# Sixty-four bytes ahead of the activations: moving the SBUF addresses of a two-block transformer kernel

## The chip, the cores and the metric

The kernel runs on one core of one Trainium2 chip. The metric is the device time of one execution in microseconds (us), as the median of three runs. Differences of well under one per cent matter here, because the runs of the kernel agree within 0.15%.

## The reference: what is computed

Two transformer blocks of two layers each are applied to one sequence of 256 tokens with 1024 channels, in float32:

```
first block, 2 layers:   x = x + rmsnorm(mix1(rmsnorm(x)))    # retention, short conv, 31-tap conv, gated
                         x = x + rmsnorm(ffn1(rmsnorm(x)))    # up 1024 -> 2*2816, conv of 3, silu, down 2816 -> 1024
second block, 2 layers:  x = x + mix2(rms(x))                 # mLSTM, sparse and differential attention, gated
                         x = x + ffn0(rms(x))                 # up 1024 -> 2*2816, silu, down 2816 -> 1024
```

The mixers have a wide input projection, three branches and an output projection. By far the most arithmetic lies in products of weights with activations.

## The kernel before

Activations are kept with channels on the 128 partitions and 256 tokens along the free axis. All weights come as one stream of chunks of 128 x 1024 float32 (`wraw`, line 307, loaded by SyncE's queue, four buffers). TensorE multiplies float32 at a reduced precision in one go (type `float32r`), so each chunk is split into two float32r parts whose sum is exact: ScalarE copies the rounding (`whi`, line 326) and VectorE subtracts it (`wlo`, line 415). Activations are split in the same way into a high and a low part: `yh`/`yl` and `hh`/`hl` for the norms' outputs and branch outputs, `fh`/`fl` inside the feed-forward stages, `ckh`/`ckl` for the key/value rank. Each block of 128 x 128 weights then meets an activation tile in three matmuls, high by high, low by high and high by low, added up in PSUM:

```
todo = [(0, 0), (0, 1), (1, 0)] if len(ws) == 2 else [(0, 0)]
for j, (a, b) in enumerate(todo):
    self.mm(o, ws[a], xs[b], ...)        # mm(out, stationary, moving)
```

In this form (kind "B" of the method `job`) the 128 columns of weights are loaded into the array (LDWEIGHTS) and 256 columns of activations stream past them (MATMUL). The trace calls such a matmul `acc<-hh,whi`: the moving operand stands first, the stationary one second. A few products (kind "A", for the values of the attentions) have the roles changed: 512 columns of weights stream past 128 columns of activations, `acc<-whi,hh`. A few chunks go to TensorE unsplit, as true float32 (`acc<-yw,wraw`), and so do sums over channels (`sp<-sqt,ones`) and the small matmuls of the mixers. Every program matmul in float32 stands in the trace as two.

Tasks of the mixers and norms are interleaved with the products by estimated times of TensorE and VectorE (`side`, `spawn`), and a scheduler sets each engine's order when the program is built.

Memory in SBUF comes from pools that are laid one behind the other, each buffer at the next free byte rounded up to a multiple of 32:

```
self.wpool = ctx.enter_context(tc.tile_pool(name="weights", bufs=1))
self.cpool = ctx.enter_context(tc.tile_pool(name="consts", bufs=1))
self.xpool = ctx.enter_context(tc.tile_pool(name="state", bufs=1))
...
self.x = self.xpool.tile([P, KD, T], F32, name="x")
```

These are lines 352 to 364. In the built program the addresses (bytes in each partition) are as follows; the last column is the start modulo 128:

| pool | buffers | first byte | modulo 128 |
|---|---|---|---|
| weights | `wraw`, `whi`, `wlo`, four each of 4096 bytes | 16,512 | 0, all twelve |
| consts | tables, parameters, `ones` | 65,664 | 0 to 96 |
| state | `x`, `yh`, `yl`, `sqt`, `hh`, `hl`, `mg` | 73,408 | 64, all of them |
| of a feed-forward stage | `fh`, `fl` and temporaries | 131,776 | 64, all of them |
| of a first mixer | `dec` ... `glu`, then `yn`, `c`, ..., then `u`, `gate` | 131,776 | 64, then 32, then 96 |
| of a second mixer | `misc`, then `ckh`, `ckl`, `prob`, ..., then `dq` ... `gate` | 131,776 | 64, then 32, then 0 |

So before the change each activation that streams through TensorE in a large product starts 64 bytes past a multiple of 128 (tiles lie 1024 bytes apart), each weight at a multiple of 128, and `ckh`/`ckl` 32 bytes past one.

Of the kernel before, what the change touches and what calls it, by code (L numbers as in the profile page):

```python
# [11 lines left out]
F32 = mybir.dt.float32  # L12
# [5 lines left out]
P = 128  # L18
# [28 lines left out]
# norms after which the first chunks of weights and what they meet go unsplit  # L47
WHOLE = (1, 2, 3, 4)
# tiles of a product that ends a chain, the last ones apart
COLUMNS = ((0, 2), (2, 2), (4, 2), (6, 1), (7, 1))  # L50
# gates and products of the branches, in their order
# [8 lines left out]
def ffn_up(arr, l):  # L60
    """Gate and value tiles side by side; the first two products take four tiles."""
    t = [[_cols(i * P, P), _cols(FF + i * P, P)] for i in range(KF)]
    return [(arr, (l,), "B", KD, c) for c in [t[0] + t[1], t[2] + t[3]] + t[4:]]


def plan():
    """The weights in the order in which the tensor engine takes them: (array, index, kind,
    k tiles, columns), kind "B" by column tiles of 128 and "A" by rows of 512."""
    jobs = []

    def seg(arr, idx, nk, off, n, step=256):
        for i in range(0, n, step):
            jobs.append((arr, idx, "B", nk, [_cols(off + i + j, P) for j in range(0, step, P)]))

    def last_singly(arr, idx, nk):
        seg(arr, idx, nk, 0, D - 256)
        seg(arr, idx, nk, D - 256, 256, P)

    for l in range(DEPTH):
        seg("w_in", (l,), KD, OFF1["cfb"], 512, 512)  # L80
        seg("w_in", (l,), KD, OFF1["cfa"], 512, 512)
        for s, n in (("q", 256), ("k", 256)):
            seg("w_in", (l,), KD, OFF1[s], n)
        jobs.append(("w_in", (l,), "A", KD, _cols(OFF1["v"], 512)))
        for s, n in (("scc", 512), ("scx", 512), ("scb", 512), ("g", 512)):
            seg("w_in", (l,), KD, OFF1[s], n)
        for what, b in BRANCHES1:
            if what == "g":
                seg("w_in", (l,), KD, OFF1["gate"] + b * D, D)
            else:  # L90
                seg(("w_ret_out", "w_sc_out", "w_cf_out")[b], (l,), 4, 0, D)
        last_singly("w_o", (l,), KD)
        jobs += ffn_up("w_up", l)
        last_singly("w_down", (l,), KF)
    for l in range(DEPTH):
        w = "w_in_2"
        misc = np.full(P, -1)
        misc[:64] = _cols(OFF2["ik"], 64)
        misc[64:72] = _cols(OFF2["mif"], 8)
        misc[72:76] = _cols(OFF2["iw"], 4)  # L100
        jobs.append((w, (l,), "B", KD, [_cols(OFF2[s] + j, P) for s in ("iq", "ckv") for j in (0, P)]))
        seg(w, (l,), KD, OFF2["mqk"], 512, 512)
        jobs.append((w, (l,), "B", KD, [misc]))
        seg(w, (l,), KD, OFF2["mqk"] + 512, 512)
        jobs.append((w, (l,), "A", KD, _cols(OFF2["mv"], 512)))
        seg(w, (l,), KD, OFF2["mo"], 512)
        seg(w, (l,), KD, OFF2["dq"], 512)
        seg(w, (l,), KD, OFF2["dk"], 512)
        jobs.append((w, (l,), "A", KD, _cols(OFF2["dv"], 512)))
        seg("dsa_w_kv_up_2", (l,), 2, 0, 512)  # L110
        jobs.append(("dsa_w_kv_up_2", (l,), "A", 2, _cols(512, 512)))
        seg(w, (l,), KD, OFF2["sq"], 512)
        for what, b in BRANCHES2:
            if what == "g":
                seg(w, (l,), KD, OFF2["gate"] + b * D, D)
            else:
                seg("w_branch_2", (l, b), 4, 0, D)
        seg("w_out_2", (l,), KD, 0, D)
        jobs += ffn_up("w_gate_up_2", l)
        if l + 1 < DEPTH:  # L120
            seg("w_down_2", (l,), KF, 0, D)
        else:
            last_singly("w_down_2", (l,), KF)
    return jobs
# [48 lines left out]
def pack_params(inputs=None):  # L173
    """Per-channel parameters, channels on partitions: (offsets, array)."""
    off, parts = {}, []
# [37 lines left out]
def make_consts():  # L213
    """Tables that depend on shapes alone: (offsets, array [128, n])."""
    off, parts = {}, []
# [55 lines left out]
def whole_chunks():  # L271
    """The chunks that go to the tensor engine as float32, unsplit."""
    out, n, i = set(), 0, 0
    for _, _, kind, nk, cols in plan():
        if kind == "B" and len(cols) == 4:
            if i // 2 in WHOLE:
                out.add(n // CB)
            i += 1
        n += nk * (len(cols) if kind == "B" else 4)
    return out  # L280


class Weights:
    """The stream of weights: loads ahead, then each chunk as the sum of two float32r parts."""
# [13 lines left out]
    def cuts(self, c):  # L298
        """The first chunk comes in halves."""
# [44 lines left out]
class Gen:  # L344
    SLACK = 4000

    def __init__(self, ctx, tc, aps):
# [15 lines left out]
        self.idle = None  # L363
        self.x = self.xpool.tile([P, KD, T], F32, name="x")
# [82 lines left out]
    def split(self, hi, lo, src):  # L447
        """src as the sum of its float32r rounding and of the exact rest."""
# [3 lines left out]
    def behind(self, engine):  # L452
        """What is traced here is issued after the engine's last urgent instruction."""
# [21 lines left out]
    def side(self):  # L475
        """Steps of the tasks beside the products, as far as the vector engine keeps up."""
# [13 lines left out]
    def job(self, evac, mov, needs=(), scale=None, last=False, spare=None):  # L490
        """The next product of the plan. mov(k) gives the two parts of the activations' tile k;
        scale, per token, is for activations that were not normalised yet; spare gives tiles."""
# [3 lines left out]
        if kind == "B":  # L496
            n = len(cols)
            accs = [self.acc() for _ in range(-(-n // 2))]
            if self.idle is not None:
                # only to keep the tensor engine's clock up while it waits  # L500
# [4 lines left out]
            for k in range(nk):  # L505
                xs = mov(k)
                for t in range(n):
# [4 lines left out]
                    # a start clears the marks of its whole bank: the first product of a bank has it  # L512
# [32 lines left out]
    def swap(self, out, src):  # L545
        """src with the halves of each 64 channels exchanged"""
# [3 lines left out]
    def rows(self, r):  # L550
        # r in DRAM, from where a row goes to many partitions
# [4 lines left out]
    def spread(self, out, row):  # L556
        """a row on all the partitions of out"""
        self.nc.sync.dma_start(out, row.to_broadcast(list(out.shape)))

# [31 lines left out]
    def rstd(self, pool, ps, scale, name):  # L591
        """1 / sqrt(scale * ps + eps)"""
# [6 lines left out]
    def sumsq(self, out, last, hold):  # L599
        """Over channels, on every partition: the sum of the squares of the eight tiles, which it  # L600
        takes by pairs, the last two also one by one (send). The first ones are added up before.
        With hold the tensor engine gets them together at the end."""
# [37 lines left out]
    def start_norm(self, g, l, folded=4):  # L640
        """Takes x by pairs of tiles (feed) for a norm whose scale per token comes last."""
# [20 lines left out]
    def end_norm(self, sd=None):  # L662
        """What the first products take, with their scale, and what the others take."""
# [38 lines left out]
    def branches(self, order, bufs, pool, mov, gate_load, needs, ys, done):  # L702
        """The sum over branches of gate * (branch output times its matrix), as two parts. A gate
        sigmoid(z) comes as tanh(z / 2), its double less 1."""
# [31 lines left out]
    def post_norm(self, zg, sums, gpre, l):  # L736
        """x += normalised zg; then the next norm's input. With s the root mean square of z, what
        the norm sees is u = s * x + zg, s times the new x."""
# [23 lines left out]
    def unscale(self, sd):  # L762
        """x out of u"""
# [10 lines left out]
    def out_proj(self, mov, g, l):  # L774
        """Four products whose columns are scaled by g, with the sum of their squares."""
# [11 lines left out]
    def first_mix(self, l, norm):  # L787
        dmov, rs, whole, mov = norm
        nc = self.nc
        with ExitStack() as st:  # L790
# [6 lines left out]
            def new_y(b):  # L797
                """Buffers for a branch's output, once those of the one before last are free."""
# [13 lines left out]
            # conformer convolution  # L812
# [65 lines left out]
            # retention  # L878
# [44 lines left out]
            # short convolution  # L923
# [133 lines left out]
    def residual(self, mov, gpre, l):  # L1057
        """x += four products; then the next norm's input."""
# [17 lines left out]
    def second_mix(self, l, norm):  # L1076
        dmov, rs, whole, mov = norm
        nc = self.nc
        with ExitStack() as st:
# [11 lines left out]
            def new_y(b):  # L1091
                """Buffers for a branch's output, once those of the one before last are free."""
# [14 lines left out]
            def rope(o):  # L1107
                """Rotates two tiles in place."""
# [6 lines left out]
            # indexer  # L1115
# [63 lines left out]
            # key/value rank  # L1179
# [33 lines left out]
            def q_task(sqs, dst, rq):  # L1213
                """rotation of the queries, and their scale per token and head"""
# [39 lines left out]
            # mLSTM queries and keys  # L1254
# [29 lines left out]
            # mLSTM gates  # L1284
# [102 lines left out]
            # attention with a softmax: sets of (queries, keys) of 64 channels  # L1387
            def softmax_group(q, k, rq, t, grp, bias, p, sums):
                """p = exp(scores - max) for the queries of tile t, sums its row sums. A group is
                sets in the same half of the partitions, one a tile."""  # L1390
# [22 lines left out]
            def transposed(p):  # L1413
                """p by keys: for each set its blocks of keys"""
# [18 lines left out]
            def ahead(q, k, rq, t, bias):  # L1433
                """The groups of tile t with their softmax, one group ahead."""
# [49 lines left out]
            def diff(l=l):  # L1484
                init = 0.8 - 0.6 * math.exp(-0.3 * l)
                for t in range(2):
                    yt = tl([P, 512], "yt", tag="yt", bufs=3)
                    for (half, tiles), p, sums in ahead(dq, dk, rq_d, t, None):
# [5 lines left out]
                        # both maps in one, up to the first one's sums  # L1494
# [44 lines left out]
            # differential attention  # L1539
# [22 lines left out]
            # sparse attention: keys and values out of the rank  # L1562
# [72 lines left out]
```

## Time and profile before

| | |
|---|---|
| median of 3 runs (lowest to highest) | 1789.89 us (1788.43 to 1791.16) |
| profiled execution, first to last instruction | 1789.1 us |
| TensorE (PE), matmuls | 1777.4 us busy, 99%, 14462 instructions |
| PE's weight loads (PEld) | 1729.2 us busy, 97% |
| VectorE (DVE) | 1363.0 us, 76% |
| ScalarE (ACT) | 1111.0 us, 62% |
| GpSimd (POOL) | 70.2 us, 4% |
| DMA | 322.52 MB, 180 GB/s in the mean |

The profiled execution's own time is its span; the median of the runs is 0.8 us longer, which covers what lies around the instructions and the scatter of the runs. Matmuls are pipelined, so the duration of one (about 280 ns) says little; what counts is the distance from the start of one to the start of the next. It is read from a long unbroken piece of the chain, as its length divided by its count, or from starts in the timeline.

### The profile page before, as it was taken

The page shows a single profiled execution, that of the slowest core. Times are in us where ns is not written, and L with a number is a line of the kernel's source. Part 1 is how long each engine was busy: PE and PEld are TensorE (multiplying, and loading weights), DVE is VectorE, ACT ScalarE, POOL GpSimd, SP SyncE. Part 2 cuts the span into 40 slices and gives each one's busy share as a digit, 9 for nine tenths or more (in the row PEclk, how much of TensorE's full clock was granted, in tenths as well). Part 3 has the DMA queues.
Part 4 walks back from the last instruction along what each step waited for, and adds up shares of the span by engine and source line. Part 5 has one row for each costly group of instructions (what it writes and reads, how often), then busy time and mean ns, then how long its engine had stood idle before and what let it go on. Part 6 is the DMA issues. An engine that isn't in the chain of part 4 may idle for free.

```text
span 1789.1 us, 35765 instructions
## 1 busy us (share of the span) xinstructions
PE 1777.4 (99%) x14462; PEld 1729.2 (97%) x14462; DVE 1363.0 (76%) x2082; ACT 1111.0 (62%) x1787; POOL 70.2 (4%) x144
## 2 busy tenths in 40 slices
PE   8999999999999999999999999999999999999999
PEld 8999999999999999999998999999999999999999
DVE  8988679865999769884887877865569887677553
ACT  7575468755666567765576666654457666655542
POOL 0000000000000000000022100000000310000000
PEclk9999999999999999999999999999999999999999
DMA  7555546554655546555465644565555664356663
GB/s 265 191 171 179 187 154 200 188 187 164 210 168 188 177 138 204 189 189 188 137 195 177 201 142 139 168 207 194 189 186 180 199 201 139 124 177 200 193 196 132
DMA packets 94648, 322.52 MB, mean 180 GB/s; under 512 B 12257, under 2 KB 16913, under 8 KB 94482
## 3 DMA queue, kind: packets, MB, share of 16 engines
q1 hardware_dynamic: 91010, 314.15, 53.9%
q0 software_dynamic: 3328, 6.09, 1.1%
q8 instruction: 113, 1.85, 0.4%
q14 instruction: 53, 0.43, 0.1%
q10 hardware_dynamic: 144, 0.00, 0.0%
HBM read 312.80 MB, written 1.10 MB: 175 GB/s over the span
## 4 chain that ended last, share of the span: by engine, by line
PE 97%; DVE 1%; DMA 1%; issue 0%; ACT 0%; POOL 0%; SPq 0%; DVEq 0%; ACTq 0%; POOLq 0%
PE acc L403 90%; PE sp L403 6%; PE sp L408 1%; DMA tmp<-dq 0%; DMA Wm<-rows 0%; DMA x<-x 0%; DVE wlo L415 0%; DVE sc L1167 0%; DVE x L415 0%; DVE m L1166 0%; DVE yw L420 0%; ACT sd L445 0%; DVE dq L415 0%; ACT whi L326 0%; POOL tmp L548 0%
## 5 line engine op out<-in xcount | busy, mean ns | idle before, releaser
L326 ACT ACTIVATE whi<-wraw 128x1024 fp32r<-128x1024 f32 (+1 forms) x575 | 606.7, 1057 | 535.9 <-PE acc L403 367.8
L415 DVE TENSOR_TENSOR wlo<-wraw,whi 128x1024 fp32r<-128x1024 f32 (+1 forms) x575 | 699.0, 1220 | 282.9 <-ACT whi L326 281.3
L403 PE MATMUL acc<-hh,whi 128*128 128x256 f32 x2832 | 791.4, 280 | 0.0
L403 PE MATMUL acc<-hl,whi 128*128 128x256 f32 x2832 | 790.8, 280 | 0.0
L403 PE MATMUL acc<-hh,wlo 128*128 128x256 f32 x2832 | 789.9, 280 | 0.0
L403 PEld LDWEIGHTS acc<-hh,whi 128*128 128x128 f32 x2832 | 531.0, 188 | 5.5 <-issue 3.7
L403 PEld LDWEIGHTS acc<-hl,whi 128*128 128x128 f32 x2832 | 531.7, 188 | 1.9 <-issue 1.2
L403 PEld LDWEIGHTS acc<-hh,wlo 128*128 128x128 f32 x2832 | 531.4, 188 | 1.1 <-issue 0.8
L403 PE MATMUL acc<-yh,whi 128*128 128x256 f32 x1280 | 269.7, 284 | 6.2 <-ACT whi L326 6.2
L403 PE MATMUL acc<-yh,wlo 128*128 128x256 f32 x832 | 231.3, 283 | 0.0
L403 PEld LDWEIGHTS acc<-yh,whi 128*128 128x128 f32 x1280 | 210.5, 190 | 7.1 <-ACT whi L326 6.2
L403 PE MATMUL acc<-fh,wlo 128*128 128x256 f32 x704 | 196.0, 278 | 0.0
L403 PE MATMUL acc<-fl,whi 128*128 128x256 f32 x704 | 195.6, 278 | 0.0
L403 PE MATMUL acc<-fh,whi 128*128 128x256 f32 x704 | 195.5, 278 | 0.0
L403 PEld LDWEIGHTS acc<-yh,wlo 128*128 128x128 f32 x832 | 155.8, 189 | 0.4
L403 PEld LDWEIGHTS acc<-fh,wlo 128*128 128x128 f32 x704 | 132.3, 188 | 0.0
L403 PEld LDWEIGHTS acc<-fl,whi 128*128 128x128 f32 x704 | 132.2, 188 | 0.0
L403 PEld LDWEIGHTS acc<-fh,whi 128*128 128x128 f32 x704 | 132.0, 188 | 0.0
L403 PE MATMUL acc<-yl,whi 128*128 128x256 f32 x384 | 108.2, 282 | 0.0
L403 PEld LDWEIGHTS acc<-yl,whi 128*128 128x128 f32 x384 | 72.1, 188 | 0.2
L445 ACT ACT_TABLE_LOAD x50 | 64.2, 1283 | 5.5 <-DVE Wm L426 3.0
L420 DVE SCALAR_TENSOR_TENSOR up<-z,prm,up 128x254 f32<-128x254 f32 (+1 forms) x128 | 55.3, 479 | 0.0
(282 smaller groups left out, 1815.2 us busy)
## 6 DMA issues: line engine op xcount, KB each, us to landing
wraw<-stream SPq DMA_DIRECT2D x581, 512.0 KB, 3.6
kr<-rows SPq DMA_DIRECT2D x32, 64.0 KB, 3.0
dec<-decay SPq DMA_DIRECT2D x2, 768.0 KB, 4.3
x<-x SPq DMA_DIRECT2D x4, 256.0 KB, 6.3
rf<-rows SPq DMA_DIRECT2D x8, 128.0 KB, 3.5
tmp<-dq POOLq DMA_DIRECT2D x16, 64.0 KB, 3.8
Wm<-rows SPq DMA_DIRECT2D x8, 128.0 KB, 3.6
tmp<-dk POOLq DMA_DIRECT2D x16, 64.0 KB, 3.9
```

The source lines that it names most:

```text
L326: nc.scalar.activation(h[:, s], r[:, s], AF.Copy)
L403: return self.nc.tensor.matmul(out, lhsT, rhs, start=start, stop=stop, **kw)
L408: return self.nc.tensor.transpose(out, in_, self.c("ident")[:k, :k])
L415: self.recent = self.nc.vector.tensor_tensor(out=out, in0=a, in1=b, op=op)
L420: return self.nc.vector.scalar_tensor_tensor(out, a, s, b, op0=op0, op1=op1)
L445: return self.nc.scalar.activation(out, in_, f, **kw)
```

## The change

One tile of 16 float32 per partition is put in front of `x`, the first tile of the pool `state`. Nothing reads or writes it. In the built program the address of every buffer of the pool `state` and of all pools behind it is 64 bytes higher: `x` starts at 73,472 instead of 73,408, and the feed-forward and mixer pools at 131,840 instead of 131,776. So `yh`, `yl`, `sqt`, `hh`, `hl`, `mg`, `fh`, `fl` lie at multiples of 128; `ckh` and `ckl` at 96 past one; what stood at 96 now stands at 32, and what stood at 0 in the second mixers (`dq` ... `gate`) at 64. The weights and the constants stay where they are. The instructions of all engines, their order and their waits are the same in both programs, one by one; only addresses differ. The rest of the diff takes out comments and shifts line numbers by two.

```
         self.t_x = [None]
         self.urgent = {}
         self.idle = None
+
+        self.xpool.tile([P, 16], F32, name="pad")
         self.x = self.xpool.tile([P, KD, T], F32, name="x")
```

## Rows read from the trace of the kernel before

**Rows 1.** The page: span, busy time of the engines, the chain by engine.
```profile
span 1789.1 us, 35765 instructions
PE 1777.4 (99%) x14462; PEld 1729.2 (97%) x14462; DVE 1363.0 (76%) x2082; ACT 1111.0 (62%) x1787; POOL 70.2 (4%) x144
...
PE 97%; DVE 1%; DMA 1%; issue 0%; ACT 0%; POOL 0%; SPq 0%; DVEq 0%; ACTq 0%; POOLq 0%
```

**Rows 2.** Groups of matmuls by form: count, busy us, mean ns, idle before.
```profile
L403 PE MATMUL acc<-hh,whi 128*128 128x256 f32 x2832 | 791.4, 280 | 0.0
...
L403 PE MATMUL acc<-yh,whi 128*128 128x256 f32 x1280 | 269.7, 284 | 6.2 <-ACT whi L326 6.2
L403 PE MATMUL acc<-yh,wlo 128*128 128x256 f32 x832 | 231.3, 283 | 0.0
L403 PE MATMUL acc<-fh,wlo 128*128 128x256 f32 x704 | 196.0, 278 | 0.0
...
L403 PE MATMUL acc<-yl,whi 128*128 128x256 f32 x384 | 108.2, 282 | 0.0
...
L403 PE MATMUL acc<-ckh,whi 128*128 128x256 f32 x16 | 4.8, 299 | 0.0
```

**Rows 3.** Chain in order of time, long pieces: start us, us, what.
```profile
169.86 66.31 PE acc L403 x563
...
251.65 177.61 PE acc L403 x1508
...
675.74 177.61 PE acc L403 x1508
...
1150.37 166.84 PE acc L403 x1472
...
1343.51 10.54 PE acc L403 x93
...
1613.05 172.40 PE acc L403 x1521
```

**Rows 4.** Windows: length, busy us (count) of each engine, PE's clock, DMA.
```profile
core 0: us, PE busy (x) PEld busy (x) DVE busy (x) ACT busy (x) POOL busy (x), PEclk, DMA share, GB/s
700.00:800.00 100.00, 100.00 (x852) 100.00 (x851) 88.36 (x152) 78.09 (x144) 0.00 (x0) 1.00 0.59 191
...
1160.00:1260.00 100.00, 100.00 (x885) 100.00 (x884) 62.59 (x84) 51.07 (x78) 0.00 (x0) 1.00 0.63 200
```

**Rows 5.** Timeline of PE across two float32 passes: start us, us, instruction.
```profile
1316.36 0.28 PE L403 MATMUL acc<-fh,wlo 128*128 128x256 f32 x1
...
1316.92 0.28 PE L403 MATMUL acc<-fl,whi 128*128 128x256 f32 x1
1317.04 0.60 PE L403 MATMUL sp<-sqt,ones 128*128 128x256 f32 x2
...
1317.59 0.28 PE L403 MATMUL acc<-fh,whi 128*128 128x256 f32 x1
...
1318.18 0.28 PE L403 MATMUL acc<-fh,wlo 128*128 128x256 f32 x1
```

**Rows 6.** Timeline of PE, moving operand 32 bytes past a multiple of 128.
```profile
967.00 0.28 PE L403 MATMUL acc<-ckh,wlo 128*128 128x256 f32 x1
...
968.78 0.28 PE L403 MATMUL acc<-ckh,wlo 128*128 128x256 f32 x1
```

**Rows 7.** Timeline of PE, weights moving, 512 columns from a multiple of 128.
```profile
45.31 0.40 PE L403 MATMUL acc<-whi,hh 128*128 128x512 f32 x1
...
47.41 0.40 PE L403 MATMUL acc<-whi,hh 128*128 128x512 f32 x1
```

**Rows 8.** Timeline of PE, eleven passes of unsplit float32.
```profile
857.80 2.54 PE L403 MATMUL acc<-yw,wraw 128*128 128x256 f32 x11
```

**Rows 9.** Groups of DVE and ACT by form, 480 to 860 us.
```profile
L415 DVE TENSOR_TENSOR wlo<-wraw,whi 128x1024 fp32r<-128x1024 f32 x123 | 149.9, 1222 | 55.9 <-ACT whi L326 55.6
...
L415 DVE TENSOR_TENSOR c<-c,tap 128x1024 f32<-128x1024 f32 x13 | 15.8, 1218 | 0.0
L445 ACT ACTIVATE z<-acc 128x512 f32<-128x512 f32 x18 | 10.4, 580 | 0.0
L445 ACT ACTIVATE gate<-acc 128x512 f32<-128x512 f32 x12 | 7.0, 579 | 0.0
```

More of the change, by code (lines that the diff above doesn't have):

```diff
@@ L363, in __init__ @@
         self.idle = None
+        self.xpool.tile([P, 16], F32, name="pad")
         self.x = self.xpool.tile([P, KD, T], F32, name="x")
```

## The prediction

> **What bounds the kernel now.** I read the page first. TensorE is busy for 1777.4 of 1789.1 us and the chain that ends last is 97% PE [rows 1]: time can be won or lost only in the distance between one matmul and the next. VectorE is idle for a quarter of the span and ScalarE for more than a third; a change of a per cent in either is absorbed.
>
> The groups by form come next: which matmuls are these? Three products with `hh`/`hl` of 2832 each, `yh,whi` 1280, `yh,wlo` 832, `yl,whi` 384, three with `fh`/`fl` of 704 each and three with `ckh`/`ckl` of 16 each [rows 2]. That is 8496 + 2496 + 2112 + 48 = 13,152 matmuls of 256 columns in float32r. At roughly 117 ns apiece they are about 1,540 us, so a nanosecond more or less in this one distance is 13 us, or 0.7%.
>
> Then I took long pieces of the chain, in which nothing else stands, and divided. Here is what the reader is to see: there are two levels. 177.61 us / 1508 = 117.78 ns, twice over, in both feed-forward stages of the first block, and 66.31 / 563 = 117.78 in its first mixer; but 166.84 / 1472 = 113.34, 172.40 / 1521 = 113.35 and 10.54 / 93 = 113.3 in the second block [rows 3]. It is the same instruction with the same forms. The granted clock is 1.00 (2.4 GHz) in a window of either level, and DMA carries 191 GB/s at the one and 200 GB/s at the other [rows 4], so neither clock nor DMA makes the difference. ScalarE and VectorE are busier where the level is high, 78 and 88 us of 100 against 51 and 63. But the level does not come and go with them within a piece: it steps at a point. In the timeline the five distances from 1316.36 to 1316.92 take 0.56 us, 112 ns each by starts that are rounded to 10 ns; two float32 passes for a sum of squares follow at 1317.04, and from 1317.59 to 1318.18 five distances take 0.59 us, 118 ns each [rows 5]; of each six starts the first and the last are shown. Same tiles `fh` and `fl`, same addresses, same engines beside it. The streams thus have at least two steady rhythms of weight load and matmul, and a break decides into which one they fall.
>
> How far are both from a bound? A float32 pass takes two clocks a column: (2.54 - 0.38) / 10 = 216 ns for 256 columns (0.38 is about the length of the last pass) [rows 8]. Half of it, 108 ns, is what 256 columns need at one clock a column. The split streams lose 5.3 ns at the low level and 9.8 ns at the high one. Something in the reading of operands is not quite free, and it is there that addresses can matter.
>
> **The change, part by part.** No instruction comes, goes or moves, and no wait changes. What changes is one property: moving operands of all 13,104 large products start at 0 modulo 128 instead of 64, with the weights still at 0.
>
> *VectorE and ScalarE.* A subtraction of 128 x 1024 takes 1222 ns with its operands at 0 (`wraw`, `whi`) and 1218 ns at 32 (`c`, `tap`); a copy of 128 x 512 out of PSUM takes 580 ns to `z` at 64 and 579 ns to `gate` at 96 [rows 9]. Within 0.3% the start does not count, and both have idle time to hide that. Cost: nothing. If this cover were gone, 0.3% of 1222 ns on some 570 splits of weights would be 2 us.
>
> *Float32 passes and small matmuls.* `yw` and `sqt` move from 64 to 0. At 216 ns per pass they stand at two clocks a column already [rows 8]. Cost: nothing; no nearer row tells of a loss.
>
> *The streams.* No row shows a stream of 256 columns with both operands at multiples of 128, so this is bounded from both sides. Below: 108 ns, the bound above. With 9,700 matmuls at the high level and 3,270 at the low one that would give 9,700 x 9.78 + 3,270 x 5.34 = 94.9 + 17.5 = 112 us. (The counts: 13,152 less the 1472 + 1521 + 93 in long low pieces is 10,066; I estimate that 370 of these stand beside another kind of work or in short low pieces, nearly half of them in each, so 9,700 high and some 3,270 low.) Above: the only streams with another start, `ckh`/`ckl` at 32, take from 967.00 to 968.78 fifteen distances, 1.78 / 15 = 118.7 ns [rows 6]. This shows that the start is not indifferent: it is above both levels found at 64. All streams at 118.7 would cost 9,700 x 0.92 + 3,270 x 5.36 = 8.9 + 17.5 = 26 us. Between them stands a row of a moving operand at 0, though of another shape and with its stationary operand at 64: nine distances of 512 columns in 2.10 us, 233.3 ns [rows 7], or 116.7 per 256 columns.
>
> Which value? From 32 to 64 the distance goes from 118.7 to 117.8 or 113.3: the rounder start is the faster one, and at 64 the low rhythm already exists and holds for 1521 matmuls without a break. I take it that with both operands at 0 the streams fall into the low rhythm and stay there: 9,700 x (117.78 - 113.34) = 9,700 x 4.44 = 43 us saved. Of the low 3,270 nothing changes.
>
> The Trainium skill speaks against this. Its page "SBUF — State Buffer" (section Specifications (TRN2)) gives 16 bytes as the line of SBUF; by it 32, 64 and 0 would all be as good, since all are multiples of 16, and the sum would be 0. The trace does not quite agree: the fifteen distances at 32 stand above those at 64.
>
> What is late next, once 43 us are gone? ScalarE waits for TensorE and not the other way round in the splits, TensorE's whole wait for `whi` is 6.2 us, at the start [rows 2], and the low level already runs with DMA at 200 GB/s [rows 4]. VectorE's 88.36 us per 852 matmuls would meet a window of 96.5 us: 92% busy, still room. So nothing takes the place.
>
> Sum: 1789.1 - 43 = 1746 us for the span, and with the 0.8 us between span and median 1747 us.
>
> **The rivals.**
>
> *A: nothing happens.* Levels are chosen by the phase in which a stream starts after a break, and one address shows both [rows 5]; 64 bytes may be a whole period of whatever is read. Then every break lands as before, since the instructions are the same: 1790 us. The same time follows if the streams go to the middle value of rows 7, 116.7: 9,700 x 1.1 saved, 3,270 x 3.3 lost, 0 in sum. For it: row by row, what fixes the level is not the start alone. Against it: the streams at 32.
>
> *B: breaks land anew, partly to the good.* If the phases change but both rhythms remain, some of the high pieces become low. Each feed-forward stage of the first block is worth 1508 x 4.44 = 6.7 us, the rest of the high ones 30 us. If the two low stages turn high (2,993 x 4.44 = 13.3 us lost) and all others low, 43 - 13.3 = 30 us are won in sum. So the case spans 1755 to 1785 us, about 1775 if only the two high feed-forward stages turn.
>
> *C: slower, the low rhythm is lost.* The low level stands almost wholly in the two feed-forward stages of the second block, 1472 + 1521 matmuls [rows 3]. If after the shift these start in the high rhythm, as the stages of the first block do, and no other gains, it costs 3,270 x 4.44 = 14.5 us: 1804 us. It decides from the point where more matmuls turn high than low. For it: three quarters of the streams are high now, so the high rhythm is what a break mostly leads to. Against it: for the same reason there is three times more to win than to lose. In the worst of it the streams take the 118.7 of rows 6: 1816 us.
>
> *D: both stalls go* and streams near 108 ns: 1678 us. For it nothing in the rows but that float32 passes reach this rate.
>
> **How the numbers follow.** No change means within 0.2%, 3.6 us, about what can be told apart here. The forecast, nearly all streams low, gets 0.35; B 0.12; D and values between it and the forecast 0.05; A 0.27, its middle value included; C 0.21, of it 0.06 for 118.7 or worse. Faster is 0.35 + 0.12 + 0.05 = 0.52, same 0.27, slower 0.21. The range takes in the forecast with a little below it, B, A and the price of C: 1742 to 1806 us; outside are D (0.05), the worst of C (0.06) and a few per cent for the unknown. Within the forecast's own case it is 1742 to 1754.
>
> **What would show it.** Right: the two long pieces of the first block's feed-forward stages shrink from 177.61 us to 1508 x 113.34 = 170.9 us, those of the second block keep 166.8 and 172.4 us, and the fall in span is 9,700 times the fall per matmul. Wrong: pieces at 117.78 still in the first block (A, B), at 117.78 in the second (C), or a third level; also wrong would be a gain that stands in waits and not in the distance of matmuls, or VectorE and ScalarE groups that change by more than 1%.

## The result

The changed kernel takes 1822.45 us (median of four runs, 1819.98 to 1824.79) against 1790.53 us of the kernel before on the same chip (1788.43 to 1791.22). The ratio is 1.018, 95% interval 1.0168 to 1.0192: it is slower by about 32 us. The forecast of 1747 us had the wrong sign, and the result lies above the range.

### The profile page after: what moved, and what is told of

It is laid out like the page before. It is cut to its first block, busy times and chain, and to the rows that moved or that the text cites. A ratio compares the mean times of both kernels' runs of the same rounds, so it can differ in the third digit from the quotient of the medians.

```text
span 1818.2 us, 35765 instructions
## 1 busy us (share of the span) xinstructions
PE 1807.2 (99%) x14462; PEld 1760.1 (97%) x14462; DVE 1363.9 (75%) x2082; ACT 1110.9 (61%) x1787; POOL 69.3 (4%) x144
## 4 chain that ended last, share of the span: by engine, by line
PE 99%; DVE 0%; ACT 0%; DMA 0%; issue 0%
PE acc L405 92%; PE sp L405 6%; PE sp L410 1%; DMA x<-x 0%; DVE x L417 0%; DVE yw L422 0%; ACT sd L447 0%; ACT yh L447 0%; ACT sqt L447 0%; ACT whi L326 0%
## 5 line engine op out<-in xcount | busy, mean ns | idle before, releaser
L405 PE MATMUL acc<-hl,whi 128*128 128x256 f32 x2832 | 799.5, 283 | 0.0
L405 PE MATMUL acc<-hh,wlo 128*128 128x256 f32 x2832 | 798.9, 283 | 0.0
L405 PE MATMUL acc<-yh,whi 128*128 128x256 f32 x1280 | 273.7, 287 | 6.4 <-ACT whi L326 6.4
```

The lines of the kernel that those rows point to most:

```text
L405: return self.nc.tensor.matmul(out, lhsT, rhs, start=start, stop=stop, **kw)
```

## The profile after

The page first: span, busy time of the engines, and further down the chain by engine (lines of the source are two higher than before).

```profile
span 1818.2 us, 35765 instructions
PE 1807.2 (99%) x14462; PEld 1760.1 (97%) x14462; DVE 1363.9 (75%) x2082; ACT 1110.9 (61%) x1787; POOL 69.3 (4%) x144
...
PE 99%; DVE 0%; ACT 0%; DMA 0%; issue 0%
```

Against [rows 1] the instructions are as many, VectorE and ScalarE are busy as long as before to within 1 us, and TensorE is busy 29.8 us longer in a span that is 29.1 us longer. The time stands in TensorE and nowhere else. The groups of matmuls by form (count, busy us, mean ns, idle before) say that no new wait came, and which forms grew:

```profile
L405 PE MATMUL acc<-hh,whi 128*128 128x256 f32 x2832 | 798.8, 283 | 0.0
L405 PE MATMUL acc<-yh,whi 128*128 128x256 f32 x1280 | 273.7, 287 | 6.4 <-ACT whi L326 6.4
...
L405 PE MATMUL acc<-fh,wlo 128*128 128x256 f32 x704 | 198.8, 283 | 0.0
```

The only idle time before these groups is the 6.4 us at the start, 6.2 before [rows 2]; the mean duration is 3 to 5 ns up. Durations of pipelined matmuls say little, so next comes the chain in order of time (start us, us, what), the same six pieces as in [rows 3]:

```profile
171.64 67.56 PE acc L405 x563
...
254.69 178.95 PE acc L405 x1508
...
682.92 178.95 PE acc L405 x1508
...
1159.45 174.68 PE acc L405 x1472
...
1360.77 11.03 PE acc L405 x93
...
1632.10 182.53 PE acc L405 x1521
```

67.56 / 563 = 120.0 ns, 178.95 / 1508 = 118.67 twice, 174.68 / 1472 = 118.67, 11.03 / 93 = 118.6 and 182.53 / 1521 = 120.0. Before they were 117.78 or 113.34. Both old rhythms are gone, the low one and the high one, and two slower ones stand in their place. Summed over all 12,850 distances from one of these streams to the next, the mean went from 116.63 to 119.08 ns: 2.45 ns x 12,850 = 31.5 us; the rest of the chain is some 2 us shorter, which leaves the 29.1 us.

Clock and DMA are no reason. The windows over the two feed-forward stages (length, busy us and count of PE, PEld, DVE, ACT, POOL, then PE's clock, DMA share, GB/s) show the full clock, 2.4 GHz, as [rows 4] do, and fewer matmuls in 100 us with both engines beside them less busy:

```profile
710.00:810.00 100.00, 100.00 (x845) 100.00 (x844) 87.67 (x152) 76.46 (x139) 0.00 (x0) 1.00 0.56 187
1170.00:1270.00 100.00, 100.00 (x845) 100.00 (x844) 58.92 (x80) 48.95 (x74) 0.00 (x0) 1.00 0.58 190
```

The two float32 passes at which the level had stepped up in [rows 5] stand here at 1333.97 (timeline of PE: start us, us, instruction):

```profile
1333.38 0.28 PE L405 MATMUL acc<-fh,whi 128*128 128x256 f32 x1
...
1333.85 0.28 PE L405 MATMUL acc<-fl,whi 128*128 128x256 f32 x1
1333.97 0.59 PE L405 MATMUL sp<-sqt,ones 128*128 128x256 f32 x2
...
1334.52 0.28 PE L405 MATMUL acc<-fh,whi 128*128 128x256 f32 x1
...
1337.96 0.28 PE L405 MATMUL acc<-fh,wlo 128*128 128x256 f32 x1
```

Four distances of 0.47 us in sum before them are about 118 ns each, and 29 distances of 3.44 us behind them are 118.6: no step here.

What was costed at nothing cost nothing. The 512 columns of moving weights take nine distances from 45.76 to 47.85 us, 232.2 ns each (233.3 in [rows 7]); the unsplit float32 passes (2.97 - 0.38) / 12 = 216 ns, as in [rows 8]:

```profile
45.76 0.39 PE L405 MATMUL acc<-whi,hh 128*128 128x512 f32 x1
...
47.85 0.40 PE L405 MATMUL acc<-whi,hh 128*128 128x512 f32 x1
...
866.11 2.97 PE L405 MATMUL acc<-yw,wraw 128*128 128x256 f32 x13
...
974.57 0.28 PE L405 MATMUL acc<-ckh,wlo 128*128 128x256 f32 x1
...
976.34 0.28 PE L405 MATMUL acc<-ckh,wlo 128*128 128x256 f32 x1
```

The last two rows answer to [rows 6]: fifteen distances in 1.77 us, 118.0 ns, with `ckh` at 96 past a multiple of 128 where 32 past one gave 118.7.

And the groups of VectorE and ScalarE that [rows 9] showed stand within 2 ns of what they were:

```profile
L417 DVE TENSOR_TENSOR wlo<-wraw,whi 128x1024 fp32r<-128x1024 f32 x123 | 149.8, 1220 | 59.0 <-ACT whi L326 58.4
...
L417 DVE TENSOR_TENSOR c<-c,tap 128x1024 f32<-128x1024 f32 x13 | 15.8, 1217 | 0.0
```

```profile
L447 ACT ACTIVATE z<-acc 128x512 f32<-128x512 f32 x18 | 10.4, 579 | 0.0
...
L447 ACT ACTIVATE gate<-acc 128x512 f32<-128x512 f32 x12 | 7.0, 580 | 0.0
```

## The experiments

Theories, as the expectations call them. R: the distance of the moving operand's start from the weights' start decides which rhythms there are. M: the moving operand's own start decides. L: any new layout deals the rhythms anew. Later T and P: what counts is the distance to the weights that are loaded beside the stream, or to the stream's own weights. Ratios are to the kernel before on the same chip, with 95% intervals. "Apart" is the start of the activations less the start of the weights; it is 64 bytes before, modulo 128 and modulo 256 alike, and 128 modulo 256 after.

### Is it the start, or the distance? (e1, e2)

e1 undoes the change and puts the pad ahead of the weights instead, so that activations lie at 0 as after and weights at 64; e2 has both pads, so that nothing is at 0 but the distance is that of after.

```
+        self.wpool.tile([P, 16], F32, name="padw")     # e1 and e2
+        self.xpool.tile([P, 16], F32, name="pad")      # e2 alone
```

> Activations at 0 modulo 128 as in the changed kernel, but the weights moved to 64: the two operands of a matmul lie 64 bytes apart again. Theory R (what counts is the start of the moving operand against that of the weights, modulo 128): the rhythms of the kernel before come back, 113.3 and 117.8 ns, and about 1790 us. Theory M (the moving operand's own start counts, and 0 is bad): 118.7 and 120 ns as after the change, about 1822 us. Theory L (every layout deals the breaks anew, without a law): any time from 1750 to 1825 us, with both of the old rhythms somewhere in it.

> Weights and activations both at 64 modulo 128, so 0 bytes apart. Theory R: 118.7 and 120 ns, about 1822 us. Theory M: as before the change, 113.3 and 117.8 ns, about 1790 us. Theory L: any time from 1750 to 1825 us.

e1: 1790.90 us, ratio 0.9999 (0.9990 to 1.0008). e2: 1826.62 us, ratio 1.0194 (1.0179 to 1.0210). The long pieces of e1's chain:

```profile
251.36 177.61 PE acc L404 x1508
...
675.57 177.61 PE acc L404 x1508
1150.51 166.84 PE acc L404 x1472
```

Their lengths are those of [rows 3] to the last digit, with the activations where after has them. In e2 the same stages take 180.96, 178.95 and 176.64 us (120.0, 118.67 and 120.0 ns). M has fallen: activations at a multiple of 128 are as good as at 64, if the weights stand 64 bytes away. R holds for starts that are moved together by 64, and L has no support, since e1's new addresses dealt every long piece as before. The distance gives the set of rhythms, not each piece's choice among them: e2 has after's distance, and yet two of these three stages are at 120.0 where after had 118.67.

### Other distances (e3, e4, e7)

Pads of 32, 128 and 256 bytes in place of the 64.

```
+        self.xpool.tile([P, n], F32, name="pad")       # e3: n = 8, e4: n = 32, e7: n = 64
```

> Weights at 0, activations at 96 modulo 128 (ahead of them 32 bytes in place of 64). Theory R in its narrow form (only 64 apart is good): 118.7 to 120 ns, 1815 to 1830 us, as the streams with ckh and ckl had at 32. In a wide form (the cost grows with the distance from 64 apart): between, some 1805 us. Theory L: any time from 1750 to 1825 us.

> 128 bytes ahead of the activations in place of 64: they lie at 64 modulo 128 again, but a whole 128 further. Theories R and M with a period of 128 bytes: 113.3 and 117.8 ns and 1790 us, within 0.3%. If the period is 256 bytes or more, the time is another one, as with the 64 bytes some 1822 us. Theory L: any time from 1750 to 1825 us.

> 256 bytes ahead of the activations: 64 modulo 128, and 64 modulo 256 against the weights as before the change (128 bytes had made that 192, and the breaks then led to the low rhythm more often). If the landing of the breaks has a period of 256 bytes: piece by piece the rhythms of before, 1790 us within 0.2%. If it has a longer period: other pieces low, 1770 to 1800 us.

e3 (96 apart): 1832.97 us, ratio 1.0232 (1.0217 to 1.0247); 98% of the streams in long pieces stand at 120.0 ns, one level, the slowest of these runs, and just above the range that narrow R gave. e4 (192 apart): 1783.63 us, ratio 0.9956 (0.9942 to 0.9970), outside the 0.3% that a period of 128 allowed. e7 (320 apart): 1790.29 us, ratio 1.0000 (0.9990 to 1.0009), all pieces as before. So 256 more change nothing, while 128 more keep both rhythms and deal them otherwise. Long pieces of e4's chain:

```profile
667.93 177.61 PE acc L404 x1508
...
1139.91 166.86 PE acc L404 x1472
...
1596.89 179.15 PE acc L404 x1521
```

The last stage went from 113.35 to 179.15 / 1521 = 117.78 ns, and yet more of the shorter pieces are low than before: of some 12,800 matmuls in pieces of twenty or more, about 5,640 are low (3,300 before). This is the prediction's picture of breaks that choose between two rhythms, at a layout where the two exist.

### Which pair of operands? (e6)

e6 moves only the low parts: `wlo` to 64, and `yl`, `hl`, `fl` to 0, by pads between the tiles. Then high by high is 64 apart, and of the other products each is 0 apart (modulo 128; modulo 256 it is 64 or 192, and 0 or 128).

```
+            if not self.parts:
+                self.g.wpool.tile([P, 16], F32, name="padw")   # ahead of the first wlo
 ...                                                            # and pads of 16 around yl, hl, fl
```

> High parts as before the change (weights whi at 0, activations yh, hh, fh at 64), low parts exchanged: wlo at 64, yl, hl, fl at 0. While one matmul streams, the weights of the next are loaded: the pairs in time are xh beside whi (64 apart), xl beside wlo (64 apart), xh beside the next whi (64 apart). The pairs that are multiplied are xh with whi (64 apart), xl with whi (0 apart), xh with wlo (0 apart). Theory T (stream and the load beside it, in time): all good, 113.3 and 117.8 ns, 1780 to 1795 us. Theory P (stream and its own weights): two of three bad, near 118.7 to 120 ns, 1810 to 1825 us. A theory of each buffer's own start, low parts at 0: 1800 us or more.

1807.35 us, ratio 1.0098 (1.0081 to 1.0115): neither of the ranges that the two theories gave. The stages of 1508 take 178.09 us, 118.1 ns, that of 1472 takes 173.82, also 118.1, and there is no low rhythm. With mixed distances the stream has a rhythm of its own; T and P both fail as stated.

### The streams alone (e11)

A kernel of its own runs only such matmuls, 300 in a row on fixed data, with all other engines idle, for moving operands at several bytes past a multiple of 256 and weights `wa` at 0; a break of a few float32 matmuls stands ahead of each.

```
mov = {o: make(..., 512, o) for o in range(0, 144, 16)}      # ma at 0, mb at 16, ... mi at 128
w = {o: make(..., 1024, o) for o in (0, 64)}                 # wa at 0, we at 64
for o in range(0, 144, 16):
    brk(2 + rep); stream([(mov[o], w[0])], 300)
```

> Not the two blocks: only streams of 300 float32r matmuls of 256 columns, one after the other, each after two or three float32 matmuls as a break; the output is the input's copy, so its time is read as that of the streams alone. In the names the letter is the start in steps of 16 bytes (ma 0, mb 16, ..., mi 128; mz 192; wa 0, we 64). Theory R: ma,wa and me,we and mi,wa 118.7 to 120 ns; me,wa and ma,we 113.3 or 117.8 ns; the steps between as the kernels with 48 and 80 apart, about 118 and 120.5 ns. If ScalarE, VectorE or DMA had a part in it, all streams would be alike here, without them. Two streams alternate two pairs: (ma,wa)(me,we) is multiplied 0 apart and loaded beside the stream 64 apart; (me,wa)(ma,we) the reverse. Theory T (stream and the load beside it): the first 113.3 or 117.8, the second 118.7 or more. Theory P (stream and its own weights): the reverse. 512 columns: 0 apart and 64 apart differ by less per column if only the load is in it. Short streams of 60 at 64 and 192 apart: both rhythms, the low one in some.

From its timeline (start us, us, matmuls), the first pass and one row of the second:

```profile
87.20 35.35 PE L59 MATMUL acc<-mc,wa 128*128 128x256 f32 x300
...
159.43 34.35 PE L59 MATMUL acc<-me,wa 128*128 128x256 f32 x300
...
231.15 36.35 PE L59 MATMUL acc<-mg,wa 128*128 128x256 f32 x300
...
268.01 34.41 PE L59 MATMUL acc<-mh,wa 128*128 128x256 f32 x300
...
339.80 36.35 PE L59 MATMUL acc<-me,we 128*128 128x256 f32 x300
...
632.31 35.68 PE L59 MATMUL acc<-me,wa 128*128 128x256 f32 x300
```

The distances by starts, once settled, are read without the first one of each stream (some 0.31 us) and the last matmul's own 0.28 us, as in (35.35 - 0.31 - 0.28) / 298 = 116.6. They are 116.67 at 32 apart (`mc`), 113.33 at 64 (`me,wa`), 120.0 at 96 (`mg`) and 113.33 at 112 (`mh`). `me,we` has the same moving operand as `me,wa` and weights 64 bytes further on: 0 apart, 120.0. The second pass of `me,wa`, behind another break, holds 117.78 for all of its 300. So the four levels of the two programs, 113.33, 117.78, 118.66 and 120.0, all come out of TensorE and its two operands; DMA, VectorE and ScalarE need have no part in the levels (VectorE, ScalarE and GpSimd are busy for 0.00 us from 480 to 880 us). The rest of the rows: 120.0 at 0 apart in both passes, 118.66 at 16, 118.3 at 48, 120.0 at 80, and 120.0, then 118.66 at 128, which is the distance after the change.

At 64 apart the rhythm is dealt by the break and then kept. At 112 apart both passes fell to 113.33, after a few matmuls at 114 to 121. That made this distance the candidate. Of eight short streams each, 64 apart had one low and 192 apart five, as in e4. The length of the break alone does not choose: of two streams 64 apart, each behind four float32 passes, one was high and one low. The two alternating streams speak neither for T nor for P: multiplied 0 apart and loaded beside 64 or 192 apart they hold 116.7 in both passes, the reverse 116.7 and then 120.0.

### Using it: distances of 48, 80 and 112, first try (e9, e10, e14, e15)

The weight tiles get 128 bytes more and are used from some floats in: the distance is 48 (e9), 80 (e10) and 112 (e14); e15 is the changed kernel itself with weights 16 bytes in, which also comes to 112, all modulo 128.

```
-            h = self.g.wpool.tile([P, CW], F32R, name="whi", tag="whi", bufs=self.BUF)
+            h = self.g.wpool.tile([P, CW + 32], F32R, name="whi", tag="whi", bufs=self.BUF)[:, s:s + CW]
 ...                          # lo likewise; s = 4 (e9, e15), 28 (e10), 20 (e14)
```

> Activations at 64, split weights at 16 modulo 128, so 48 apart in place of 64. If only exactly 64 apart is good (period 128, halves of 64): between 118 and 120 ns, 1815 us or more. If the cost grows evenly from 64 to 0 or 96 apart: 1795 to 1810 us. If the best point lies below 64: under 1785 us.

> Activations at 64, split weights at 112 modulo 128, so 80 apart in place of 64. If only exactly 64 apart is good: 118 to 120 ns, 1815 us or more. If the cost grows evenly from 64 to 96 apart (1833 us there): some 1810 us. If the best point lies above 64: under 1785 us.

> Activations at 64, split weights at 80 modulo 128: 112 apart, 16 bytes short of level. In the streams alone this distance went to 113.3 ns both times, even out of a beginning at 116 to 121, while 96 and 128 apart ran at 118.7 to 120. Theory R as the streams show it (the distance modulo 128 gives the set of rhythms, and at 112 the low one draws the others in): nearly all pieces at 113.3, whatever the breaks; 11,400 streams from 117.1 to 113.4 ns are 42 us, and with the streams beside other work 45: about 1745 us. If breaks decide here too: between 1755 and 1790 us. If only full halves of 64 bytes are good in the whole kernel: 1815 us.

> The changed kernel with its activations at multiples of 128 as they are, and only the split weights moved to 16 modulo 128: again 112 apart. Theory R: the loss of the change turns into a gain, near 1745 us, with the same rhythms as the kernel with 64 and 80. If multiples of 128 for the activations were bad in themselves: 1820 us.

e9: 1803.73 us (ratio 1.0078, 1.0063 to 1.0093); e10: 1821.81 us (1.0176, 1.0160 to 1.0191); e14: 1808.81 us (1.0103, 1.0088 to 1.0118); e15: 1807.66 us (1.0097, 1.0080 to 1.0113). What the expectations had not regarded: a buffer of 4096 + 128 bytes puts every other weight buffer 128 further on modulo 256. So half of the chunks have the distance that was wanted and half another: 112 and 240 in e14 and e15 (6,528 and 6,576 of e14's large matmuls in the built program), 48 and 176 in e9, 80 and 208 in e10. e9 fell into the range of an even rise and e10 into that of exactly 64, which settles neither. e14 and e15 missed what was expected of them; their long pieces stand at 117.5 to 119.4, not at 113.3.

The half at 240 is not the whole reason. With the addresses of the built program laid beside the trace, matmul by matmul, none of e14's 208 stretches of sixteen or more matmuls 112 apart ends at 113.3, and none of e15's 204: they end at 116.6 to 120.1, the ones right behind a break too. The first and the last start of one of e15's, 48 matmuls (timeline of PE):

```profile
293.96 0.28 PE L405 MATMUL acc<-hh,whi 128*128 128x256 f32 x1
...
299.44 0.28 PE L405 MATMUL acc<-hh,wlo 128*128 128x256 f32 x1
```

These are 47 distances in 5.48 us, 116.6 ns each. Likewise e9's stretches 48 apart, all but one, end at 116.4 to 116.8, where the streams alone held 118.3. What differs is where the pair of operands stands: the streams alone had their weights at 0 modulo 256, e14 and e15 have the ones that are 112 away at 80 and 144. So the distance alone does not give the rhythms. It did in the runs with one distance throughout and weights at a multiple of 64, and in these four the weights lie 16 or 48 bytes past one.

### Finer steps, and the period (e16)

Streams alone again, by steps of four bytes around 112 and around 240, three passes.

```
mov = {o: make(..., o) for o in 96 + 4 * range(9)}           # ma at 96, ... me at 112, ... mi at 128
mov.update({o: make(..., o) for o in 224 + 4 * range(9)})    # na at 224, ... ne at 240, ... ni at 256
```

> Streams alone again (the two blocks are left out, the output is the input's copy), 100 matmuls each, three times each after one, two or three float32 matmuls, in steps of 4 bytes: ma 96, mb 100, ..., me 112, ..., mi 128, and na to ni the same 128 further; wa 0, wb 64, mk 48. Theory R with steps of 16 bytes: 96 to 108 alike at 120, 112 to 124 alike at 113.3, 128 at 118.7 or 120. With steps of 4 bytes: a level of its own each. Last, two alternating streams: first multiplied 112 apart and loaded beside the other stream 48 apart, then the reverse. Theory T: the second at 113.3, the first at 117 to 118.5. Theory P: the reverse. If both pairs count: neither at 113.3.

Third pass and, for `ne`, the first, from the timeline (start us, us, matmuls):

```profile
175.22 12.07 PE L59 MATMUL acc<-ne,wa 128*128 128x256 f32 x100
...
591.63 13.33 PE L59 MATMUL acc<-mc,wa 128*128 128x256 f32 x100
605.91 12.34 PE L59 MATMUL acc<-md,wa 128*128 128x256 f32 x100
619.19 11.71 PE L59 MATMUL acc<-me,wa 128*128 128x256 f32 x100
631.85 12.51 PE L59 MATMUL acc<-mf,wa 128*128 128x256 f32 x100
```

104 apart: 130.0 ns, alternating between 123 and 137. 108: 120.0. 112: 113.3 once settled, in all three passes. 116: 121.7. 240: 117.1. Four bytes are worth up to 10 ns, 17 of the 18 levels repeat over the three passes within 0.3 ns (120 apart within 1.3), and 240 is not 112: the period is 256, not 128, which agrees with e4 and e7. Streams whose own weights were 112 away and those beside them 48, or the other way round, held 116.7 to 117.8, neither the 113.3 of the one distance nor the 118.3 of the other (e11): both pairs count, as in e6.

### The distance of 112 in every buffer (e17)

Here the activations are moved, by whole 256 bytes of extra room in each tile and 48 bytes of offset: they stand at 240 modulo 256 in every buffer and the weights at 128.

```
+    def part(self, pool, n, name, **kw):
+        t = pool.tile([P, n * T + 64], F32R, name=name, **kw)
+        return t[:, 12:12 + n * T].rearrange("p (k t) -> p k t", k=n)
 ...                          # for hh, hl, yh, yl, fh, fl
```

> Every product's activations start 112 bytes apart from their weights modulo 256, in every buffer (activations at 240, weights at 128 modulo 256), where the streams alone fell to 113.33 ns from any start. If the distance modulo 256 sets the rhythms in the whole program as it does in streams alone (theory R), nearly all of the 11,400 spacings go to 113.3: 1790.5 - (117.08 - 113.35) x 11,400 ns = 1748 us, range 1743 to 1756. If the whole program's rhythm depends also on the distance to the weights that are loaded beside the stream (here the same 112, since all weight buffers lie alike) nothing differs from that. If only a break decides between two rhythms and the streams alone were a special case, the time lies at 1775 to 1795.

1753.36 us (four runs, 1753.19 to 1753.54), ratio 0.9791 (0.9775 to 0.9807): the fastest of all and faster than both kernels, with the same instructions. Its page and its chain:

```profile
span 1751.5 us, 35765 instructions
PE 1738.7 (99%) x14462; PEld 1690.0 (96%) x14462; DVE 1359.3 (78%) x2082; ACT 1110.5 (63%) x1787; POOL 69.9 (4%) x144
```

```profile
165.87 63.87 PE acc L403 x563
...
245.10 170.97 PE acc L403 x1508
...
655.81 170.97 PE acc L403 x1508
...
1118.95 166.89 PE acc L403 x1472
...
1575.43 172.45 PE acc L403 x1521
```

Each of these pieces is now at 113.4 ns, and all 80 pieces of twenty matmuls or more settle at 113.3 within some fifteen, whatever break stands ahead of them. Over all 12,850 distances the mean is 113.64 (116.63 before, 119.08 after): 2.99 x 12,850 = 38 us, and the span is 37.6 us shorter. At 112 apart, with the weights at 128 in every buffer, the level of the streams alone holds in the whole program. Why e14's and e15's stretches at 112 did not reach it stays open: no run has one distance of 112 throughout with weights off a multiple of 64.

### Breaks on purpose (e12, e13, e18)

The other way to the low rhythm is the break. These three (e12 and e13 ran twice each) take e4's layout and put one float32 matmul of two columns (e13: two of them) at the head of six products ahead of high stretches; e18 leaves the fifth out. They write to an accumulator that the product then starts anew.

```
+BREAKS = {29: (1, 2), 44: (1, 2), 96: (1, 2), 111: (1, 2), 172: (1, 2), 252: (1, 2)}   # e18: no 172
 ...
+            for _ in range(BREAKS.get(self.nj, (0, 0))[0]):
+                m = BREAKS[self.nj][1]
+                self.nc.tensor.matmul(accs[0][:, :m], self.ones[:, :P], self.ones[:, :m], start=True, stop=True)
```

> The layout with 128 bytes (64 modulo 128, 1783.6 us), and at the start of six products, among them the third of the feed-forward stages that were high, one more float32 matmul of 2 columns (its result is overwritten). If a break deals the rhythm anew and the rhythm then holds: the pieces behind these six points change between 113.3 and 117.8 as a whole, each long one worth 6.5 us; with half of them low some 1773 us. If the addresses alone set the rhythm: the same pieces high, 1784 us and 0.2 us each for the breaks.

> As the one before, with two float32 matmuls of 2 columns at the same six points. If breaks deal anew: another set of pieces low than with one; if all six were low, 1762 us. If the addresses alone set it: 1785 us.

> The layout of the 128-byte pad (activations 192 apart modulo 256) with five breaks of one float32 matmul of two columns, without the one at product 172, which is held to have turned the stretch of 340 from 117.78 to 113.35 and the stretch of 1,471 after it the other way. If a break only swaps the two rhythms for what follows: the stretch of 340 is back at 117.78, that of 1,471 at 113.35, and the time is 1762.3 + 340 x 4.43 ns - 1,471 x 4.43 ns = 1757 us (1755 to 1760). If the levels after a break are dealt anew with each program: anywhere from 1757 to 1775.

e12: 1762.29 us, ratio 0.9841 (0.9813 to 0.9870). e13: 1765.61 us, ratio 0.9860 (0.9831 to 0.9889), with the same long stretches low. e18: 1763.70 us, ratio 0.9842 (0.9826 to 0.9857). In e12's chain both stages of the first block are low (157.90 / 1392 = 113.4) and the stage of 1472 has become high, 117.8:

```profile
258.17 157.90 PE acc L406 x1392
...
670.39 157.90 PE acc L406 x1392
...
1119.78 173.37 PE acc L406 x1472
```

In e18's profiled execution the stage of 1472 is back at 166.86 us, as expected, and that execution took 1758.2 us, as expected. But its other three took 1763.2 to 1764.3, 5 to 6 us more, so the rhythms are not dealt alike in every execution; the stage of 1,471 distances is worth 6.5 us, but no trace shows which stretch it was. That a break can turn the rhythm is shown; that it only swaps the two is not. In e12 each of the six turned its own stretch low. The six more of e13 shift the starts by 0.2 us each, 1.4 us in sum; the rest of what e13 takes longer comes between 883 and 944 us, where no break was added and a piece of 90 went from 113.5 to 117.8 ns.

## Why the prediction was wrong

**What bounds the kernel: right.** TensorE's spacing was the whole of it, and with the same instructions the span differs by 67 us between e17 and after.

**Two rhythms, chosen at the break: right**, at distances of 64 and 192 (e4, e11, e12), though not by the break's length alone (e11).

**VectorE, ScalarE, float32 passes, moving weights: right.** All within a per cent.

**"Which value?": the step that failed.** The prediction took the moving operand's start as the variable, and from two points, 118.7 at 32 and 117.8 or 113.3 at 64, it read that "the rounder start is the faster one". On this it put 43 us saved, which came out as 31.5 us lost. Both points are of another variable. With weights at 0 a start of 64 is also a distance of 64, and e1 and e2 separate them: start 0 at distance 64 gives 113.34 and 117.78, start 64 at distance 0 modulo 128 gives 118.67 and 120. Nor is there a trend in the distance: 0, 32, 64, 96 and 112 apart give 120.0, 116.7, 113.3 or 117.8, 120.0 and 113.3 (e11). Any line through two points would have been wrong. And the point at 32 was a weak one: `ckh` lies 160 past its weights modulo 256 in the built program, and the fifteen distances stand right behind a break. In e7, with the same starts modulo 256, the same fifteen take 1.76 us, 117.3 ns, below the high level at 64 (timeline of PE):

```profile
966.75 0.28 PE L404 MATMUL acc<-ckh,wlo 128*128 128x256 f32 x1
...
968.51 0.28 PE L404 MATMUL acc<-ckh,wlo 128*128 128x256 f32 x1
```

The row called the nearest for "both at 0", the 512 columns of [rows 7], had its weights at 0 and its activations at 64: it was as far from the wanted case as the others.

**The price of the failure.** Rival C named the level, 118.7, and priced it: 9,700 x 0.92 + 3,270 x 5.36 = 26 us, 1816 us. Measured were 29 us in the trace, the rest being the pieces at 120.0, which no row showed. So the place of the result stood in the text, at a chance of 0.06. That the level fits is luck: rows 6 show another distance than after's 128, and e7 another value for them. The mechanism fits in part: the low rhythm was lost as C had it, but the high one was lost too. Two unknown ends and a row of the kernel itself above both old levels would have earned that case at least as much as the forecast.

**Rival A's "whole period"** was a fair thought with the wrong length: 256 bytes change nothing (e7), 64 and 128 do (after, e4).

**The size was nearly right.** All streams low was put at 43 us; e17 did it and gained 37. By the mean of before, (116.63 - 113.34) / 4.44 = 74% of 12,850 distances were high, 9,500, which make 42 us; and at 112 the pieces settle only after some matmuls, so that the mean stays at 113.64.

**The SBUF line.** The Trainium skill's page "SBUF — State Buffer" (section Specifications (TRN2)) gives a line of 16 bytes, from which the prediction drew that 32, 64 and 0 would be alike. Against that now stand more than fifteen matmuls: in e11, distances that are all multiples of 16 hold levels from 113.33 to 120.0 ns. The Trainium skill's same page (section Who interferes with whom) has TensorE never wait on anyone. No run here shows another engine slowing these streams, whose levels are the same with all others idle (e11); but TensorE's own two operands are not free of each other, since the same moving operand takes 113.33 or 117.78 ns, and 120.0 with weights 64 bytes further on.

**What stays open.** Why a distance has its level: no run looked inside. What the operands' own place does beside their distance, which e14 and e15 show to count. Whether the stream's own weights or those loaded beside it count: in e6 and in the alternating streams both did. Why a break leads to one rhythm at 64 apart and 112 forgets it, and why e18 differs from run to run.

## What to carry to other kernels

Where TensorE is full with back-to-back matmuls that each load new weights, divide long pieces of the chain by their counts: two levels in one form of instruction mean that time lies in spacing, and moving addresses is then a free experiment worth 2% either way here. Set it by the distance between moving operand and weights modulo 256, with the weights at a multiple of 64 as in the runs where this held, and the same in every buffer (a tile's padded size decides that as well as its start), and measure a short kernel of streams alone over the distances first, with the weights where the kernel has them, since levels cannot be guessed from roundness. When a row is to stand for an unseen case, write down every variable that differs, not the one that the change names.

## What the runs showed that was not expected

- Two steady rhythms of the same instructions at the same addresses, 113.33 and 117.78 ns, kept over 1,500 matmuls and changed at a break of two float32 passes [rows 5]; e11 has 300 in a row at each, behind breaks of four and six passes.
- Four bytes between 108 and 112 apart are 6.7 ns a matmul, and between 104 and 108 10 ns (e16).
- 112 apart, a stream falls to 113.33 ns by itself within some ten matmuls, from 114 to 121 (e11, e16), and in the whole program settles there behind every break (e17, weights at 128). With weights at 80 or 144 modulo 256 the same distance never does (e14, e15).
- No stream of 256 columns settled below 113.33 ns at the full clock. The Trainium skill's page "TensorE: Matmul & The Clock Gate" (section Back-to-back issue gap) gives N / 2.4 + 2.5 for a matmul by itself, an estimate of 109.2 ns for 256 columns, and 131 ns for 512 columns in a stream with weight loads; no run here reached either, and 512 columns took 227 to 233 ns (e11, after).
